# A hybrid decoder layer: where the second half's normalized tokens are transposed

## The chip, the cores and the metric

The kernel runs on one core of one Trainium2 chip. The metric is the device time of one launch in microseconds (us). The median of three runs of the kernel before is 2236.77 us (2235.26 to 2238.23).

## The reference, cut to what matters

Sixteen meta tokens are put ahead of 2048 tokens of 1024 channels (float32). One layer is computed on them:

```python
h = rmsnorm(x, norm_g)                     # per token, over 1024 channels
p = h @ w_in                               # 8208 columns
q, k, v = l2norm/silu of causal_dwconv(p[..., :3072])      # 8 heads x 128
o = chunk_gated_delta_rule(q, k, v, g, beta)               # state 128 x 128 a head
o_dn = rmsnorm(o) * silu(z)
o_sc = b * causal_dwconv(c * hh) * silu(sz)                # 1024 channels
out = rmsnorm(x + concat(o_dn, o_sc) @ w_out, final_g)
```

What this document is about is the first line and its way into the second: the normalized tokens have to stand with the channels on the partitions (h transposed) before the projection can contract over channels.

## The kernel before, in words

The tokens are worked in two halves of 1024 (the first with the 16 meta tokens as well). For each half the transposed, normalized tokens lie in SBUF in two tiles, HH and HL (1024 channels as 8 blocks of 128 partitions, by tokens): HH holds the values rounded to the matmul's float32r format, HL what is left over. Each projection is a "job": 128 columns of `w_in`, split in the same way into `wh` and `wl`, and 24 matmuls for each group of tokens (hh x wh, hl x wh, hh x wl, eight channel blocks each). The first half has three groups of tokens (272, 384 and 384), the second two of 512 (`groups`, lines 365 to 368). Eight slots of eight jobs make a half: q, k, v and the gate z of one head of the delta rule, and four jobs of the short convolution. The second half has the same jobs; its HH and HL are written over those of the first, group by group, once the last two jobs of the first half have read a group (`("free", g)`, line 1517).

Between the matmuls of the jobs runs the delta rule of the heads, as Python generators that are stepped by a planner: `delta_front` (decay, the matrices of key products, a substitution by VectorE), `delta_back` (transposes, the merge of the block inverses), `delta_scan` (the recurrence over eight chunks) and `delta_out`. The planner (`Model`, lines 30 to 100) holds an assumed free time for every engine and a ready time for every tile, and steps a generator when its time has come; so the order of the instructions on TensorE, VectorE, ScalarE and GpSimd is fixed when the program is built. A chip that is later than the plan waits in that order. SP, which issues all DMAs, is not among the engines whose order is fixed by hand (lines 205 to 214).

The second half's tokens are normalized while the first half runs: in each head but the last, `fresh` (line 1065) waits until the scan of the head before is done and then steps `normalize(t)` for one tile of 128 tokens (head 5 has two). `normalize` (line 518) loads the tile into the buffer "kd", takes its mean square on ScalarE (with "gw" for scratch), a power on GpSimd and three small steps on VectorE, multiplies each half of 512 channels by the root and the gain, and stores the tile in DRAM (`xnd`), still with the tokens on the partitions. `delta_back` of the same head starts only when `("fresh", i)` is set, since it uses "kd" as well. "Q" and "gw" are buffers shared with the delta rule and the gates; `hold` (line 571) keeps others off a shared buffer.

At the border `prologue1` (line 544) loads the eight tiles back through three buffers of the short convolution (`sc_c`, `sc_y`, `sc_u`) and calls `turn` (line 383) twice for each tile: four 128 x 128 transposes on TensorE into one of two PSUM buffers "ta", a ScalarE copy into HH and a VectorE subtraction into HL. These sixteen calls stand between the matmuls of the last two jobs of the first half and of the first job of the second. `run_group` (line 736) waits in the plan for `("h", hf, g)`. The weights of the second half's first two jobs are split on GpSimd (`POOLED`), all others on VectorE.

## Time and profile before

| | |
|---|---|
| median of three runs | 2236.77 us |
| profiled execution: its time, its span | 2236.26 us, 2234.5 us |
| mean granted clock of TensorE | 0.992 |
| TensorE busy | 2174.5 us |
| VectorE busy | 1451.7 us |
| ScalarE busy | 854.0 us |
| GpSimd busy | 189.3 us |
| DMA | 197.14 MB in 258366 packets on SP's queue, 46.0% of 16 engines |

The profile is one execution. In it PE is TensorE's matmuls, PEld its weight loads, DVE VectorE, ACT ScalarE, POOL GpSimd and SPq the queue of SP that issues DMAs. An instruction is named by the tiles that it writes and reads (`hl<-ta,hh` writes hl from ta and hh). All instructions have line 118, that of the helper that records them, so they are told apart by their tiles. A number in brackets behind an instruction is the time that its engine stood idle before it, with what ended the wait. The first half's projections run from some 45 us to 951 us, the second half's to some 1930 us, and the output projection fills the rest.

### The profile page before, as it was taken

Reading aid. Unit: us, or ns where it says so; the run is one execution under the profiler, and the core shown is the slowest. Engines: PE = TensorE matmul, PEld = TensorE weight load, DVE = VectorE, ACT = ScalarE, POOL = GpSimd, SP = SyncE. Lnnn points to the kernel's source line nnn. Section 1 sums busy time; section 2 is a strip of 40 time slices with the busy share of each in tenths; the row PEclk is TensorE's granted clock in tenths of the full one; section 3 lists DMA queues with packets and bytes.
Section 4 is the critical chain, followed back from the end, with each engine's and each line's share of the span. In section 5 each row is a group of like instructions: output and inputs, shape, how many; then the busy total and the mean of one; then the engine's idle time right before and its main releaser. Section 6 shows DMA issues by size and latency. Waiting matters only on the chain.

```text
span 2234.5 us, 35464 instructions
## 1 busy us (share of the span) xinstructions
PE 2174.5 (97%) x13472; PEld 1917.1 (86%) x13472; DVE 1451.7 (65%) x3919; ACT 854.0 (38%) x1987; POOL 189.3 (8%) x345
## 2 busy tenths in 40 slices
PE   6999999999998999999999999999999999999998
PEld 6999999999998999977888888888888877888886
DVE  4677777677775668686767677676767674444422
ACT  5533434343443334444344352425252523332211
POOL 4010101010101010111010101010101000000000
PEclk9999999999999999999999999999999999999999
DMA  5434544353446744523444423343677343645521
GB/s 140 76 77 67 86 70 95 64 95 65 92 61 78 83 76 89 131 43 60 82 70 65 83 57 78 53 78 53 79 52 75 60 114 126 203 170 188 188 91 57
DMA packets 258537, 199.41 MB, mean 89 GB/s; under 512 B 62117, under 2 KB 226478, under 8 KB 258366
## 3 DMA queue, kind: packets, MB, share of 16 engines
q1 hardware_dynamic: 258366, 197.14, 46.0%
q8 instruction: 106, 1.74, 0.3%
q14 instruction: 65, 0.53, 0.1%
HBM read 160.51 MB, written 36.59 MB: 88 GB/s over the span
## 4 chain that ended last, share of the span: by engine, by line
PE 88%; DMA 4%; DVE 3%; ACT 2%; SPq 1%; issue 1%; POOL 0%; POOLq 0%; ACTq 0%; DVEq 0%
PE mm L118 75%; PE ta L118 7%; PE rec L118 4%; PE o L118 2%; DMA kd<-in_x_dram 2%; SPq L118 1%; ACT junk L118 1%; DMA wr<-in_w_in_dram 1%; DMA nb<-nbd 1%; DVE prod L118 1%; DMA xtd<-XT 0%; DVE wl L118 0%; DVE XT L118 0%; ACT wh L118 0%; DVE acc L118 0%
## 5 line engine op out<-in xcount | busy, mean ns | idle before, releaser
L118 PE MATMUL mm<-hh,wh 128*128 128x512 f32 (+3 forms) x2816 | 1008.4, 366 | 8.7 <-ACT hh L118 6.7
L118 PE MATMUL mm<-hl,wh 128*128 128x512 f32 (+3 forms) x2816 | 985.4, 357 | 0.4 <-DVE hl L118 0.4
L118 PE MATMUL mm<-hh,wl 128*128 128x512 f32 (+3 forms) x2816 | 640.1, 360 | 1.7 <-DVE wl L118 1.7
L118 PEld LDWEIGHTS mm<-hh,wh 128*128 128x128 f32 x2816 | 533.1, 190 | 60.3 <-ACT hh L118 7.9
L118 PEld LDWEIGHTS mm<-hl,wh 128*128 128x128 f32 x2816 | 532.5, 190 | 48.1 <-DVE hl L118 1.9
L118 PEld LDWEIGHTS mm<-hh,wl 128*128 128x128 f32 x2816 | 479.6, 189 | 48.9 <-DVE wl L118 2.2
L118 DVE TENSOR_TENSOR wl<-wr,wh 128x512 fp32r<-128x512 f32 x356 | 238.3, 689 | 97.6 <-ACT wh L118 77.0
L118 DVE SCALAR_TENSOR_TENSOR acc<-raw,pcol,acc 128x384 f32<-128x384 f32 (+2 forms) x360 | 232.9, 649 | 87.9 <-ACT acc L118 83.8
L118 ACT ACTIVATE wh<-wr 128x1024 fp32r<-128x1024 f32 x182 | 191.9, 1055 | 88.7 <-PE mm L118 49.7
L118 DVE SCALAR_TENSOR_TENSOR prod<-nb,XT 128x8 f32<-128x8 f32 (+30 forms) x496 | 191.0, 385 | 22.7 <-DMA nb<-nbd 19.1
L118 DVE TENSOR_REDUCE XT<-prod 128x8 f32<-128x16 f32 (+30 forms) x496 | 147.2, 297 | 17.0
L118 ACT ACTIVATE vn<-rec,cj 128x128 f32<-128x128 f32 x128 | 46.9, 366 | 248.4 <-PE rec L118 248.1
L118 ACT ACTIVATE raw<-mm 128x384 f32<-128x384 f32 (+2 forms) x120 | 61.5, 513 | 192.7 <-PE mm L118 192.2
L118 PE MATMUL mm<-oh,wh 128*128 128x512 f32 x256 | 101.9, 398 | 0.0
L118 ACT ACTIVATE sc_c<-mm 128x384 f32<-128x384 f32 (+3 forms) x82 | 42.1, 515 | 154.4 <-PE mm L118 154.3
L118 PE MATMUL mm<-ol,wh 128*128 128x512 f32 x256 | 100.4, 392 | 0.0
L118 DVE SCALAR_TENSOR_TENSOR yy<-rec,neg,vr 128x128 f32<-128x128 f32 x128 | 44.5, 348 | 56.1 <-PE rec L118 55.5
L118 DVE TENSOR_TENSOR y<-mm,y 128x512 f32<-128x512 f32 x21 | 14.5, 691 | 101.1 <-PE mm L118 101.1
L118 ACT ACTIVATE ojk<-y 128x512 bf16<-128x512 f32 x21 | 13.2, 631 | 164.6 <-DVE y L118 127.1
L118 DVE SCALAR_TENSOR_TENSOR S<-S,egl,rec 128x128 f32<-128x128 f32 x104 | 35.7, 343 | 59.6 <-PE rec L118 59.1
L118 POOL TENSOR_TENSOR opy<-mo,nhalf 128x4 f32<-128x4 f32 x32 | 34.3, 1073 | 460.3 <-DVE mo L118 451.5
L118 POOL TENSOR_SCALAR_AFFINE_SELECT E<-E 128x1024 f32<-128x1024 f32 x16 | 18.3, 1143 | 641.8 <-PE ta L118 352.3
(240 smaller groups left out, 2574.4 us busy)
## 6 DMA issues: line engine op xcount, KB each, us to landing
wr<-in_w_in_dram SPq DMA_DIRECT2D x128, 512.0 KB, 7.8
wr<-mixd SPq DMA_DIRECT2D x54, 512.0 KB, 4.3
E<-gtd SPq DMA_DIRECT2D x16, 512.0 KB, 3.8
qd<-ged SPq DMA_DIRECT2D x16, 512.0 KB, 6.4
nb<-nbd SPq DMA_DIRECT2D x64, 128.0 KB, 2.8
mixd<-zs SPq DMA_DIRECT2D x32, 256.0 KB, 2.4
out_dram<-y SPq DMA_DIRECT2D x16, 512.0 KB, 2.7
kd<-in_x_dram SPq DMA_DIRECT2D x9, 512.0 KB, 7.6
```

Of the source, the lines that this page charges most:

```text
L118: r = real(*args, **kw)
```

## The change

`xnd` gets another shape: for each tile eight blocks of 128 x 128 with the channels first. `normalize` turns each half of a tile itself: a VectorE block transpose of 128 x 512 (32 x 32 blocks) into the buffer "gw", and four DMAs, each from 32 partitions in runs of 32 elements (128 B), that put the blocks in their transposed place in DRAM. It then lets `DRAIN` (4.0 us of planned time) pass before it lets go of "gw" or goes on, and it holds "gw" against the gates, which now hold it too. At the border `turn` is replaced by `split_h`, which reads the loaded tile in SBUF and has no transposes; the load takes each partition in eight runs of 512 B.

```diff
-    xnd = tc.dram_tile([NC, 128, D], F32, name="xnd")
+    xnd = tc.dram_tile([NC, KT, 128, 128], F32, name="xnd")
...
-    def turn(xt, k0, col, n):
-        pt = ptile(pta, "ta", [128, 4, 128])
-        for k in range(4):
-            kx = 4 * k0 + k
-            tr(pt[:, k, :n], xt[:, kx * 128 : kx * 128 + 128], n)
-        h_ = HH[:, 4 * k0 : 4 * k0 + 4, col : col + n]
-        l_ = HL[:, 4 * k0 : 4 * k0 + 4, col : col + n]
-        nc.scalar.activation(h_, pt[:, :, :n], AF.Copy)
-        nc.vector.tensor_tensor(out=l_, in0=pt[:, :, :n], in1=h_, op=ALU.subtract)
+    def split_h(xt, k0, col):
+        x_ = xt[:, 512 * k0 : 512 * k0 + 512].rearrange("p (k i) -> p k i", i=128)
+        h_ = HH[:, 4 * k0 : 4 * k0 + 4, col : col + 128]
+        l_ = HL[:, 4 * k0 : 4 * k0 + 4, col : col + 128]
+        nc.scalar.activation(h_, x_, AF.Copy)
+        nc.vector.tensor_tensor(out=l_, in0=x_, in1=h_, op=ALU.subtract)
...
     def normalize(i):
...
         yield after(xt)
+        yield from hold("gw")
         st = statistics(xt, 128, vt(dp, [128, 1840], "gw", dt=BF16))
...
             nc.vector.scalar_tensor_tensor(xc, xc, rs, gains[c2], op0=ALU.mult, op1=ALU.mult)
             if c2 == 0:
                 gain(1)
+            else:
+                held.discard("Q")
+            yield after(slot=(dp, "gw"))
+            yield from hold("gw", True)
+            u = vt(dp, [128, 4, 128], "gw")
+            turn_out(xnd[i, 4 * c2 : 4 * c2 + 4], xc.rearrange("p (c i) -> p c i", i=128), u)
+            yield DRAIN
+            held.discard("gw")
+            if c2 == 0:
                 yield after(gains[1])
-        held.discard("Q")
-        nc.sync.dma_start(xnd[i], xt)
         done.add(("xn", i))
...
-            nc.sync.dma_start(xts[i], xnd[i])
+            nc.sync.dma_start(
+                xts[i].rearrange("p (k i) -> p k i", i=128), xnd[i].rearrange("k p i -> p k i")
+            )
...
-                yield after(xts[i], slot=(pta, "ta"), eng="DVE", lag=1.2)
-                yield from hold()
-                turn(xts[i], k0, col, 128)
+                yield after(xts[i], eng="DVE", lag=1.2)
+                split_h(xts[i], k0, col)
...
+    def turn_out(dram, src, tmp):
+        nc.vector.transpose(out=tmp.rearrange("p c i -> p (c i)"), in_=src.rearrange("p c i -> p (c i)"))
+        for a in range(4):
+            nc.sync.dma_start(
+                dram[:, :, 32 * a : 32 * a + 32].rearrange("c (b y) x -> y (c b) x", b=4),
+                tmp[32 * a : 32 * a + 32].rearrange("y c (b x) -> y (c b) x", b=4),
+            )
...
+        yield from hold("gw", True)
         gw = vt(dp, [128, 920], "gw")
...
         nc.sync.dma_start(ged[hf, :Wd], gT[:Wd])
+        held.discard("gw")
...
+    DRAIN = 4.0
```

## Rows read from the trace of the kernel before

**Rows 1.** The page's table: busy time, share, instructions of each engine
```profile
PE 2174.5 (97%) x13472; PEld 1917.1 (86%) x13472; DVE 1451.7 (65%) x3919; ACT 854.0 (38%) x1987; POOL 189.3 (8%) x345
```

**Rows 2.** Busy us (count) by stretch: stretch, length, engines, granted clock, DMA share, GB/s
```profile
60.00:1000.00 940.00, 918.47 (x6565) 881.89 (x6564) 675.01 (x2066) 386.24 (x958) 84.79 (x154) 0.99 0.47 79
...
957.00:965.00 8.00, 7.86 (x35) 6.38 (x36) 6.13 (x25) 2.54 (x5) 1.72 (x5) 0.79 0.54 77
1000.00:1700.00 700.00, 696.65 (x4148) 577.12 (x4147) 492.79 (x1249) 283.58 (x668) 60.14 (x90) 1.00 0.45 69
```

**Rows 3.** Timeline of TensorE around one turn: start, length (us), instruction, count
```profile
935.42 0.60 PE L118 MATMUL ta<-ident,sc_y 128*128 128x128 f32 x4
935.77 0.42 PE L118 MATMUL mm<-hh,wh 128*128 128x384 f32 x1
936.03 0.34 PE L118 MATMUL mm<-hl,wh 128*128 128x384 f32 x1
936.21 0.33 PE L118 MATMUL mm<-hh,wh 128*128 128x384 f32 x1
```

**Rows 4.** Timeline of TensorE, first half's end to group 1; brackets: idle before, releaser
```profile
951.47 0.40 PE L118 MATMUL mm<-hh,wh 128*128 128x512 f32 x1
...
957.00 0.66 PE L118 MATMUL ta<-ident,sc_c 128*128 128x128 f32 x4 [2.87 <-DVE hl L118]
...
970.67 0.39 PE L118 MATMUL mm<-hh,wh 128*128 128x512 f32 x1
```

**Rows 5.** The tile hh: subtractions; ns min/median/max, first and last start
```profile
L118 DVE TENSOR_TENSOR hl<-ta,hh x16: 672/691/693, 927.6 to 963.2; 128x512 fp32r<-128x512 f32 x16
```

**Rows 6.** Timeline of GpSimd and VectorE beside that hole
```profile
949.59 2.70 POOL L118 TENSOR_TENSOR wl<-wr,wh 128x1024 fp32r<-128x1024 f32 x1 [16.39 <-ACT wh L118]
...
950.27 2.04 DVE L118 SCALAR_TENSOR_TENSOR msm<-mnb,mXT 16x5 f32<-16x5 f32 x1
```

**Rows 7.** The page's costliest groups: subtractions that read SBUF alone; mean ns
```profile
L118 DVE TENSOR_TENSOR wl<-wr,wh 128x512 fp32r<-128x512 f32 x356 | 238.3, 689 | 97.6 <-ACT wh L118 77.0
```

**Rows 8.** The tile X: VectorE's block transposes; ns min/median/max
```profile
L118 DVE STREAM_TRANSPOSE X<-W x48: 422/434/440, 209.2 to 1856.3; 32x256 f32<-32x256 f32 x48
```

**Rows 9.** Timeline of SP's queue: four short-run stores
```profile
876.91 1.82 SPq L118 DMA_DIRECT2D xtd<-XT  x4
```

**Rows 10.** DMA issues: count, KB each, median us to landing
```profile
wr<-in_w_in_dram SPq DMA_DIRECT2D x128, 512.0 KB, 7.8
...
xnd<-kd SPq DMA_DIRECT2D x8, 512.0 KB, 2.9
...
xtd<-XT SPq DMA_DIRECT2D x64, 32.0 KB, 4.2
...
sc_c<-xnd SPq DMA_DIRECT2D x3, 512.0 KB, 4.8
```

**Rows 11.** The buffer xtd, first half: its landing times
```profile
DMA to landing us min/median/max: 1.6/1.9/7.6
```

**Rows 12.** VectorE's waits, first half: us in total, times, longest
```profile
DVE pxt L118 <- POOL pxy L118: 17.3, 4, 6.5
...
DVE prod L118 <- DMA nb<-nbd: 10.2, 4, 7.1
```

**Rows 13.** Timeline of TensorE: the two waits that followed from these
```profile
699.22 0.79 PE L118 MATMUL rec<-yy,W 128*128 128x128 f32 x2 [3.63 <-DVE yy L118]
...
724.75 0.66 PE L118 MATMUL rec<-ident,os 128*128 128x128 f32 x4 [3.79 <-DVE os L118]
```

**Rows 14.** Timelines of SP, VectorE and TensorE: head 5's chain, head 7's k job
```profile
756.03 0.33 SPq L118 DMA_DIRECT2D xnd<-kd  x1
...
765.81 3.69 SPq L118 DMA_DIRECT2D xtd<-XT  x4
...
836.90 0.33 DVE L118 SCALAR_TENSOR_TENSOR Sh<-S,egl,rec 128x128 f32<-128x128 f32 x1
...
845.41 0.29 PE L118 MATMUL mm<-hh,wh 128*128 128x272 f32 x1
```

## The prediction

> **What bounds the kernel now.** I read the page's engine table first: TensorE is busy 97% of the span, the next engine, VectorE, 65% [rows 1]. The reader is to see that only time on TensorE's own queue counts, and that an edit elsewhere counts only by the waits that it gives TensorE. The table by stretches comes next: in the first half (60 to 1000 us) TensorE has 21.5 us without work, VectorE is busy 72% of it, and in the second half (1000 to 1700) TensorE lacks 3.4 us in 700 [rows 2]. So the second half follows TensorE closely, and time won at the border between the halves stays won. Then the timeline of TensorE at that border. A turn of half a token tile (four transposes) stands between the projection matmuls sixteen times [rows 3], and one of them is the longest hole there: 2.87 us, which ended with a VectorE subtraction [rows 4]. Behind the hole the granted clock is 0.79 on the mean of 8 us, against 1.00 in the second half [rows 2]; part of that stretch ran at the lower of the two levels (1.2 and not 2.4 GHz), after TensorE had stood idle.
>
> **The change part by part.** All times are those of the profiled execution: 2234.5 us of span, 2236.26 us in all, 0.5 under the median of the three runs.
>
> *Removed from TensorE.* One turn: 0.35 us from its first transpose to the next matmul, and that matmul takes 0.26 where the following step takes 0.18 [rows 3]. That is 0.43, and 16 x 0.43 = 6.9 us. All of it lies on the queue that sets the end; nothing hides it.
>
> *The hole goes.* The turn at 957.00 waited for its PSUM buffer, which VectorE's late subtraction held: 2.87 us. With no transpose there, the matmuls behind it have their inputs and run. The low clock after it goes too: (1 - 0.79) x 8.0 us = 1.7 us [rows 2]. What is late next is group 1 of the second half, whose first matmul is at 970.67 [rows 4] and needs all subtractions of tiles 5 to 7. Before, the last of them started at 963.2 and took 0.69 [rows 5], so it ended 12.4 us after the first half's last column group had let its buffer go (951.47). Ten turns lie ahead of that point, so it comes 4.3 us earlier, at 947.2; 12.4 us later is 959.6. TensorE wants it at 970.67 - 11.5 = 959.2. So even if VectorE takes as long as before, 0.4 us is lost; I count 0. If the hole only moves there, it costs again what it cost, 2.9 + 1.7.
>
> VectorE is slow there because of GpSimd: the 2.70 us weight split on GpSimd stands over a VectorE instruction of 16 x 5 elements that took 2.04 us [rows 6], and a second pair follows 4 us later. The Trainium skill, page SBUF — State Buffer, section Who interferes with whom, says that a VectorE instruction with two SBUF inputs is blocked by a GpSimd instruction that reads SBUF, and that one with a PSUM input isn't. The trace agrees with the first half. It speaks against the change, since the split's subtraction now reads its tile from SBUF and so can itself be blocked; by that rule up to 2 x 2.0 us of delay could fall on the subtractions, which would give back about 4 us at the border.
>
> *The split itself.* ScalarE's copy and VectorE's subtraction stay, 16 of each, from SBUF instead of PSUM: the subtraction from PSUM takes 691 ns, the like one from SBUF 689 [rows 5, 7]. No change; ScalarE likewise.
>
> *Added to VectorE.* Sixteen block transposes of 128 x 512. The trace has 32 x 256 at 434 ns [rows 8]. With twice the elements it lies between 0.43 (all fixed) and 0.87 (all per element); I take 0.87, so 13.9 us over eight tiles. VectorE is idle 28% of the first half, and the projection matmuls hide it: 0 on the path. If that cover fails, it costs at the rate by which VectorE's waits reach TensorE. VectorE waited 17.3 + 10.2 = 27.5 us for late powers and late block loads in the first half, and two TensorE waits, 3.63 + 3.79 = 7.4 us, came of these [rows 12, 13]. The rate is 0.27, so 3.8 us at most.
>
> *Added to SP and the DMA engines.* Per half tile four stores, 64 in all in place of 8. Four stores of the same run length (128 B) take 1.82 us to issue [rows 9], so 16 x 1.82 = 29 us of SP's queue less 8 short ones. SP waits in it for VectorE's transpose, with weight loads behind; they are asked for two jobs ahead, so 0; without that lead, 29 us at the rate above would be 7.7. The store that VectorE waits for is another matter: the second half tile's transpose writes the same buffer, so it waits until the first four stores have landed, and the whole of VectorE's queue stands behind it (scan steps, convolutions), for which TensorE waits at the rate above. The planner lets 4.0 us pass (DRAIN). Landing of the like stores is 4.2 us in the median [rows 10]; that buffer's stores and loads together took 1.6 to 7.6 in the first half [rows 11]. I take 4.2, the row of stores alone; the new ones have twice the bytes. Wait: 1.8 + 4.2 - 4.0 = 2.0 us a tile, 8 x 2.0 x 0.27 = 4.3 us. Ends: 0 (landing 1.6) and 8 x 5.4 x 0.27 = 11.7 (landing 7.6).
>
> 512 KB stored in long runs lands in 2.9 us, 32 KB in 128 B runs in 4.2 [rows 10]. The Trainium skill, DMA: Bandwidth & Descriptors, Specifications, states that below 512 B a transfer is a read-modify-write and misses line rate: the trace agrees in direction. By that rule the end near 11.7 is likelier than 0.
>
> *The loads at the border* now gather 512 B runs, as the weight loads do: 7.8 us to landing, not 4.8 [rows 10]. Only the first tile's has no turn ahead to cover it. ScalarE would wait up to 3.0 us; I take 3.0 x 0.27 = 0.8 (ends 0 and 3.0).
>
> *The normalizing stream gets longer* and delta_back waits for it ("fresh"). Each half tile adds the 4.0 drain and 0.87, so 9.7 a tile. Head 5 has two tiles: its last store, at 756.03, goes to 775.5, past the end of the substitution (765.81 + 3.69 = 769.5) [rows 14]. Head 5's scan then ends 6.0 us later than its 837.2. The slot that needs it, head 7's k job, starts at 845.41 [rows 14]: 8.2 us of slack, so 0. If the slack is gone, each us over it costs TensorE one us, at most 19.5 - 8.2 = 11.3. The other heads have one tile each (head 7 none): 9.7 us, so with no more than head 5's slack 1.5 us each, which I count at 0.
>
> **Sum:** -6.9 - 2.9 - 1.7 + 4.3 + 0.8 = -6.4 us: 2229.9 on the profiled execution, 2230.4 on the median. I forecast 2230.
>
> **Rivals.**
> *Late stores, slower.* Place: VectorE's second transpose of each tile. If landing is 7.6 us at all eight, VectorE waits 5.4, and if TensorE pays as it did for the longest block load (3.63 of 7.1, or 0.51 [rows 12, 13]), 8 x 5.4 x 0.51 = 22 us: 2236.8 - 11.5 + 0.8 + 22 = 2248. It decides from a TensorE loss of 10.7/8 = 1.34 us a tile, which is a VectorE wait of 2.6 and a landing of 4.8 us. For it: twice the bytes of the row, short runs. Against: most like landings before were near 2 us.
> *The first half takes the gain back.* Landing 7.6 at the mild rate 0.27: 2236.8 - 11.5 + 11.7 + 0.8 = 2237.8. The slack of head 7's k job used up gives the same size.
> *The hole stays (the change does not do all it says).* TensorE loses the transposes but waits at 959 for the blocked subtractions or for the late loads of tiles 5 to 7: only 6.9 won, so 2236.8 - 6.9 + 5.1 = 2235. For it: the margin there is nil.
> *Better.* Stores land within the drain, and the new order also dissolves one of the two waits of 3.6 to 3.8: 2236.8 - 11.5 - 3.7 = 2221.6. Against: nothing in the change aims at these waits.
>
> **How the numbers follow.** Forecast 0.44 (own range 2226 to 2232), better 0.14, first half takes it back 0.14, hole stays 0.10, late stores slower 0.18. About 0.2% (4.5 us) is what a measurement can tell from no change. Faster 0.44 + 0.14 = 0.58; same 0.14 + 0.10 = 0.24; slower 0.18. The range 2221 to 2245 leaves out the tip of the better case and the worse half of the slower one.
>
> **What would show it.** Right: no "ta" matmul of sc_c, sc_y or sc_u tiles between the halves, no hole and a granted clock of 1.00 there, the second half's first group at least 9 us earlier against the last one of the first, and VectorE's waits ahead of the new transposes of 2 us or less. Wrong: waits of TensorE on VectorE in the first half that sum to over 7.4 + 11 us, a wait on hh or hl before group 1, or a hole ahead of head 7's k job.

## The result, and the profile after

The changed kernel takes 2265.28 us (median of four runs, 2260.31 to 2269.35) beside 2236.33 of the kernel before on the same chip: ratio 1.0128 [1.0105, 1.015]. It is 29 us slower. I had forecast 2230, and the range ended at 2245.

Everywhere below, single stages come from one profile of each kernel. Two profiles of the same instructions can stand up to 10 us apart at a point (e12 and e13 at 819 us, ahead of all that tells them apart; after and e6, which turn out to be one program, 7.7 us at 1669), so a stage counts only where it recurs in several kernels. The medians carry the verdicts.

**The page of after.** Span 2265.0 us against 2234.5, of which TensorE is busy:

```profile
PE 2189.5 (97%) x13408; PEld 1924.6 (85%) x13408; DVE 1454.7 (64%) x3931; ACT 850.9 (38%) x1985; POOL 190.7 (8%) x345
```

The 64 transposes are gone (13408 matmuls for 13472 in [rows 1]), and yet TensorE is busy 15.0 us longer and idle 15.5 us longer (75.5 for 60.0). Busy time grows with fewer instructions when the clock is lower. The mean granted clock fell from 0.992 to 0.982. Clock loss, (1 - clock) x span with the clocks unrounded, is 40.2 us after and 17.0 before: 23 us more. The table by stretches shows where:

```profile
60.00:1000.00 940.00, 909.67 (x6420) 874.27 (x6419) 662.46 (x2040) 377.07 (x948) 84.94 (x154) 0.97 0.51 79
782.00:866.00 84.00, 78.69 (x562) 73.26 (x561) 53.52 (x176) 37.27 (x104) 8.42 (x16) 0.90 0.49 80
780.00:800.00 20.00, 19.54 (x95) 17.54 (x95) 11.50 (x24) 9.21 (x33) 1.38 (x3) 0.70 0.74 69
...
968.00:1030.00 62.00, 56.85 (x246) 41.93 (x246) 50.38 (x171) 23.41 (x44) 3.88 (x7) 0.92 0.29 47
1000.00:1700.00 700.00, 694.39 (x4077) 570.04 (x4076) 489.60 (x1234) 280.35 (x649) 54.52 (x79) 0.99 0.46 66
1660.00:1680.00 20.00, 17.85 (x145) 13.47 (x144) 9.15 (x16) 6.52 (x12) 0.19 (x1) 0.64 0.29 49
```

The granted clock is the last number but two. In the first half it is 0.97, where before had 0.99 [rows 2]. The stretches from 782, 968 and 1660 are the ones where this profile of after loses its time: (1 - 0.90) x 84 = 8.4 us of clock, 5.0 and 7.2. The kernel before ran 780 to 800 and 1660 to 1680 at 1.00 with TensorE 20.00 of 20 us busy.

**The waits ahead of those stretches.** TensorE's timeline of after (start, length, instruction; in brackets the idle time before it and who ended it), which answers to [rows 4, 13]:

```profile
715.16 0.79 PE L118 MATMUL rec<-S,k 128*128 128x128 f32 x2 [5.79 <-DVE S L118]
...
779.36 0.55 PE L118 MATMUL mm<-hh,wh 128*128 128x256 f32 x1 [4.12 <-DVE sc_y L118]
...
856.58 0.65 PE L118 MATMUL rec<-S,k 128*128 128x128 f32 x2 [1.09 <-DVE S L118]
...
945.56 0.80 PE L118 MATMUL rec<-yy,W 128*128 128x128 f32 x2 [3.11 <-DVE yy L118]
...
974.32 0.49 PE L118 MATMUL rec<-S,k 128*128 128x128 f32 x2 [1.63 <-DVE S L118]
976.15 0.75 PE L118 MATMUL rec<-yy,W 128*128 128x128 f32 x2 [1.12 <-DVE yy L118]
...
1664.97 0.22 PE L118 MATMUL ta<-X,E 32*32 32x32 f32 x2 [1.33 <-issue]
```

The hole on hl at 957.00 is gone, as forecast; these stand in its place. They are short, and where a stretch at a low clock follows, it can cost more than the wait (1660 to 1680: 2.15 us of waits, 7.2 us of clock). On S, yy, sc_y, X and wl of VectorE, TensorE waited 23.1 us between 60 and 1000 us (10.2 + 5.3 + 4.1 + 1.8 + 1.7): over the 18.4 that the prediction had named as the sign that it is wrong. By the same count before has 15.4, on os, yy, hl and wl.

**The parts that I had priced.** The tiles hl and gw and the DMA issues of after [rows 5, 8, 10], then VectorE's waits on DMAs and GpSimd over the whole span [rows 12]:

```profile
L118 DVE STREAM_TRANSPOSE gw<-kd 128x512 f32<-128x512 f32 x16 | 11.3, 708 | 1.2 <-DMA xnd<-gw 1.0
```
```profile
L118 DVE TENSOR_TENSOR hl<-sc_c,hh x6: 672/682/692, 938.0 to 976.0; 128x512 fp32r<-128x512 f32 x6
```
```profile
Q<-in_norm_g_dram SPq DMA_DIRECT2D x16, 256.0 KB, 3.9
...
xnd<-gw SPq DMA_DIRECT2D x64, 64.0 KB, 3.0
```
```profile
DVE prod L118 <- DMA nb<-nbd: 26.3, 7, 9.6
DVE kd L118 <- DMA Q<-in_norm_g_dram: 19.3, 4, 10.5
...
DVE gw L118 <- DMA xnd<-gw: 1.0, 2, 0.6
DVE pxt L118 <- POOL pxy L118: 0.3, 1, 0.3
```

The wait that I priced highest, VectorE on the landing of the first four stores, is 1.0 us in all, not 8 x 2.0. In its place VectorE waits 19.3 us, in four waits, for the second gain load, which it had hardly waited for before. The block transpose takes 0.71 us.

**Head 5's chain** [rows 14], SP's queue and VectorE's timeline of after:

```profile
754.79 4.01 SPq L118 DMA_DIRECT2D wr<-in_w_in_dram  x2
760.87 0.35 SPq L118 DMA_DIRECT2D Q<-in_norm_g_dram  x1
761.62 19.36 SPq L118 DMA_DIRECT2D xnd<-gw  x8
```
```profile
747.71 0.75 DVE L118 SCALAR_TENSOR_TENSOR kd<-kd,pxr,Q 128x512 f32<-128x512 f32 x1 [5.74 <-DMA Q<-in_norm_g_dram]
...
776.35 0.75 DVE L118 SCALAR_TENSOR_TENSOR kd<-kd,pxr,Q 128x512 f32<-128x512 f32 x1 [10.48 <-DMA Q<-in_norm_g_dram]
```

The last store of head 5's second tile is issued by 781, against 756.03. I had worked out 775.5 with 2.2 us to spare; the two waits on gain loads, 16.2 us, were not in it. The second of these gain loads is issued at 760.87, right behind two weight loads, and lands at 776.33, 15.5 us later, where 3.9 is the median of such loads. In before, SP's queue has it ahead of the weight load:

```profile
750.54 0.33 SPq L118 DMA_DIRECT2D Q<-in_norm_g_dram  x1
754.60 0.38 SPq L118 DMA_DIRECT2D wr<-in_w_in_dram  x1
```

The scans, counted by ScalarE's vn, are 11.8 to 16.8 us late at the starts of heads 1 to 4, 23.2 at head 5's and 28.5 at head 6's, and TensorE waits for them from 853 to 859 and from 974 to 982 us.

**How stages are lined up.** ScalarE's 120 records of acc (one per column group of q, k or v that leaves TensorE) are complete in every profile, so the shift of the n-th against before tells how late a kernel is there. Where an order moves other work across such a point, a part of the shift is that work and no loss. The stages in the expectations were lined up by a count of TensorE's mm records that was not complete (every trace holds 9296 of them) and drifted: they put 16 us on after's stage from 782 to 850 us, where the table has 8.2 from 819 to 948. The table is the corrected one. Shifts in us; the columns are the time in before.

| kernel | 726 | 819 | 948 | 971 | 1070 | 1611 | 1669 | span |
|---|---|---|---|---|---|---|---|---|
| after | +1.6 | +3.8 | +12.0 | +19.6 | +18.1 | +21.5 | +30.5 | +30.5 |
| e1_border_only | +3.0 | +3.3 | -2.6 | -2.8 | -9.3 | +1.0 | +11.1 | +3.9 |
| e8_quarter_turns | +3.1 | +3.5 | -1.4 | -2.2 | +1.2 | +6.3 | +5.7 | +9.0 |
| e2_first_half_only | -2.0 | +2.0 | +9.7 | +11.5 | +13.7 | +16.0 | +21.2 | +14.9 |
| e3_spread | +7.8 | +1.5 | +2.5 | +10.5 | +9.0 | +13.3 | +26.7 | +20.2 |
| e4_gains_first | +6.0 | +7.9 | +13.6 | +21.4 | +20.7 | +30.6 | +33.2 | +35.8 |
| e6_no_drain | -0.8 | +3.2 | +12.2 | +19.7 | +18.3 | +21.7 | +22.8 | +27.1 |
| e7_long_runs | +1.0 | +4.3 | +13.4 | +21.6 | +20.3 | +23.7 | +23.9 | +21.9 |
| e5_before_spread | -3.6 | -4.9 | -6.2 | -6.3 | -5.1 | -1.0 | +10.3 | +3.7 |
| e15_spread_order_kept | -0.1 | +0.1 | -2.7 | -2.7 | +0.1 | +4.4 | +15.6 | +10.6 |
| e9_border_order_kept | +5.2 | +6.3 | +3.1 | +4.5 | +7.2 | +7.2 | +7.7 | +5.7 |
| e16_border_small_turns | +3.9 | +2.2 | +1.6 | +1.3 | +1.3 | +2.0 | +1.6 | +1.6 |
| e12_no_lows | +5.6 | +9.6 | +5.4 | -0.5 | +1.1 | +1.1 | +1.4 | +1.8 |
| e13_before_no_lows | -0.1 | +0.1 | -0.2 | -5.2 | -3.6 | -3.5 | -3.9 | -3.7 |
| e11_first_order_kept | +3.2 | +5.3 | +5.3 | +6.3 | +9.1 | +9.9 | +9.3 | +7.3 |
| e10_all_order_kept | +6.7 | +10.0 | +6.7 | +7.1 | +7.1 | +7.1 | +8.6 | +7.6 |
| e18_all_small_turns | +2.7 | +2.4 | +1.8 | +1.5 | +4.2 | +4.6 | +6.8 | +10.9 |
| e14_lows_on_pool | +8.1 | +11.3 | +10.6 | +14.2 | +14.2 | +14.2 | +15.5 | +17.6 |
| e17_before_extra_turns | +1.7 | +1.1 | +12.0 | +15.9 | +17.6 | +17.5 | +16.9 | +16.2 |

After loses 8.2 us from 819 to 948, 7.6 at the border and 9.0 from 1611 to 1669. The first two are there in e6 and e7 as well, which have after's order, and the third is not. The first thing that the table shows is that the second half runs in step once the order of before is kept: in the nine kernels of its last rows, from e9 on, the shift at 1070 is still there at 1611, within 0.8.

### The profile page after: what moved, and what is told of

It is laid out like the page before. It is cut to its first block, busy times and chain, and to the rows that moved or that the text cites. A ratio compares the mean times of both kernels' runs of the same rounds, so it can differ in the third digit from the quotient of the medians.

```text
span 2265.0 us, 35410 instructions
## 1 busy us (share of the span) xinstructions
PE 2189.5 (97%) x13408; PEld 1924.6 (85%) x13408; DVE 1454.7 (64%) x3931; ACT 850.9 (38%) x1985; POOL 190.7 (8%) x345
## 3 DMA queue, kind: packets, MB, share of 16 engines
q8 instruction: 105, 1.72, 0.3%
## 4 chain that ended last, share of the span: by engine, by line
PE 87%; DMA 5%; DVE 3%; ACT 2%; SPq 2%; issue 1%; POOL 0%; POOLq 0%; DVEq 0%; ACTq 0%
PE mm L118 74%; PE ta L118 7%; PE rec L118 4%; PE o L118 2%; SPq L118 2%; DMA nb<-nbd 1%; ACT junk L118 1%; DMA wr<-in_w_in_dram 1%; DMA xnd<-gw 1%; DMA sc_y<-xnd 0%; DVE prod L118 0%; DVE acc L118 0%; DVE wl L118 0%; DVE hl L118 0%; DMA W<-xtd 0%
## 5 line engine op out<-in xcount | busy, mean ns | idle before, releaser
L118 PE MATMUL mm<-hh,wh 128*128 128x512 f32 (+3 forms) x2816 | 1009.5, 366 | 16.8 <-ACT hh L118 11.3
L118 ACT ACTIVATE ojk<-y 128x512 bf16<-128x512 f32 x22 | 13.9, 631 | 174.0 <-DVE y L118 127.2
L118 ACT ACTIVATE acc<-mm,pcol 128x384 f32<-128x384 f32 (+2 forms) x120 | 71.9, 599 | 0.0
L118 POOL TENSOR_TENSOR kpy<-ssk,nhalf 128x8 f32<-128x8 f32 x16 | 28.2, 1764 | 516.3 <-DVE ssk L118 454.0
```

Source lines behind the costliest of these rows:

```text
L118: r = real(*args, **kw)
```

## The experiments

Medians; "before" is the kernel before on the same chip (2236.1 to 2237.8).

**First: which half of the change costs it?** Theory A: the longer normalizing makes head 5 late. Theory B: the short-run stores hold up the loads beside them.

*e1_border_only*: the kernel before with the split from SBUF in place of the turn, and its plain store and load.

```diff
-                turn(xts[i], k0, col, 128)
+                split_h(xts[i], k0, col)
```


> The kernel before, with only the border changed: tiles are normalized, stored and loaded as before (not transposed; so the second half is computed from tokens whose blocks are not turned), and split_h takes the place of turn. No short-run stores, no longer normalizing stream. Theory A (the longer normalizing stream makes head 5's chain late) and theory B (the short-run stores hold up the gain and block loads) both put the whole loss into the first half, so both expect the border's gain alone: 2236.3 - 6.9 (transposes) - 4.6 (hole and low clock) = about 2225, and no hole of over 1 us at the border. If the border itself is at fault, this stays at 2236 or above.

Measured 2242.41, ratio 1.0025 [1.0015, 1.0035]: 17 us above what I expected. The half that had to win, alone, loses. At 1070 us it is 9.3 us ahead; from 1070 to 1669 it loses 20. Some 7 us of both are work that its order puts off: between the two records next to 1070 and 1611 us TensorE is busy 548.1 us in e1 and 540.7 in before, both at a clock of 1.00. From 1669 to the end 7.2 us come back.

*e2_first_half_only*: the normalizing of after with its stores to a place that nothing reads, beside the plain store; the border of before.

```diff
+            turn_out(xnd[i, 4 * c2 : 4 * c2 + 4], ..., u)
+            yield DRAIN
...
+        nc.sync.dma_start(xnp[i], xt)
...
-            nc.sync.dma_start(xts[i], xnd[i])
+            nc.sync.dma_start(xts[i], xnp[i])
```


> The changed kernel with the border of before: the transposes and the 64 short-run stores are made (into DRAM that nobody reads), and the tile is also stored as before, loaded as before and turned by TensorE. Theories A and B: the whole loss stays and the border's gain is missing, so 2265 + 7 to 11 = 2272 to 2276, with TensorE's hole ahead of head 7's k job. If the loss comes from the border, about 2236 to 2242.

Measured 2250.76, 1.0073 [1.0056, 1.009]: the first half costs 14 us alone, less than expected. 14.3 + 6.0 is not 29, so the halves don't simply add.

*e3_spread*: after, with no head that normalizes two tiles but head 0.

```diff
-            news = ((0,), (1,), (2,), (3,), (4,), (5, 6), (7,), ())[i] if hf == 0 else ()
+            news = ((0, 1), (2,), (3,), (4,), (5,), (6,), (7,), ())[i] if hf == 0 else ()
```


> The changed kernel with the second tile moved from head 5 to head 0 (tiles 0 and 1 in head 0, then one in each head up to 6), so that no head but the first, which has about 40 us of cover, normalizes two. Same instructions, same stores. Theory A: head 5's scan ends at about 845 or earlier instead of 860, TensorE's waits there and the low clock go, -13 to -16 us: about 2250. Theory B: same stores, same late loads, so within 5 us of 2265.

Measured 2256.34, 1.0096 [1.0081, 1.0111]: 9 us under after. The loss from 819 to 948 falls from 8.2 to 1.0, as theory A says; the 8.0 at 948 to 971 and 13.4 from 1611 stay.

*e4_gains_first*: after, with both halves of a tile scaled before either is transposed.

```diff
+                yield after(gains[1])
+        held.discard("Q")
+        for c2 in range(2):
+            xc = xt[:, 512 * c2 : 512 * c2 + 512]
```


> The changed kernel with both halves of a tile scaled first and both transposes and their stores after them, so that the second half's gain is loaded ahead of the stores. Theory B: VectorE's waits for the gain load fall from 19.3 us to under 2, and the time to about 2255. Theory A: the stream is as long as before (only the waits inside move), head 5 is as late, 2262 to 2268.

Measured 2272.75, 1.0179 [1.0156, 1.0201]: 7 us slower than after. VectorE's waits on gain loads fell to 8.3 us and it gained nothing by it. But the order is another one too, so this does not clear the gain loads.

**Second: the order.** What stands out is that kernels which differ little lose at places where nothing of theirs was changed. Every instruction is placed by the planner's own clock, so one edit moves all behind it. Theory C: the new order is what costs.

*e5_before_spread*: the kernel before with e3's table (the same one-line edit).

> The kernel before, with nothing but the places of its normalized tiles moved as in e3_spread: head 0 takes two tiles, heads 1 to 6 one each, instead of two at head 5. Theory A (in the kernel after, the longer normalizing at head 5 uses up the slack of head 7's k job; in the kernel before, that slack is there): no change, 2232 to 2238 us, since the stage from 782 to 850 us has only 0.8 us of idle to give. Theory C (any new order of the instructions breaks up the order of before and makes new short waits of TensorE, each followed by a stretch at the lower clock): slower by 0.3% or more, 2243 to 2256 us, like the parts of e3_spread that lie outside that stage.

Measured 2238.31, 1.0 [0.999, 1.0011]. A new order need not cost. But a loss from 1611 to 1669 is there (+11.3), in a kernel without any part of the change, and up to 1070 it is ahead. From 1669 to the end 6.6 us of it come back.

*e6_no_drain*: after without the pauses.

```diff
-    DRAIN = 4.0
+    DRAIN = 0.0
```


> The kernel after, with the pause of 4 us that each half of a tile keeps behind its stores set to 0, so that a tile's normalizing is up to 8 us shorter and gives the buffer gw back before its stores have landed. Theory A (length of the normalizing stream at head 5): head 5's two tiles end 16 us earlier, the stage from 782 to 850 us falls from +16 us to under +5, the time to about 2250 to 2255 us; who takes gw next waits up to 3 us for the stores. Theory B (the stores' traffic delays the loads of gains and blocks): the same traffic, only earlier, 2260 to 2270 us. Theory C (the order alone): anywhere from 2255 to 2275 us, with the loss moved to other stages.

Measured 2262.96, 1.0116 [1.0098, 1.0134]. The edit moved nothing: in the traces of e6 and of after, the instructions of all four engines and SP's DMAs stand in the same order (13408 on TensorE, 3931 on VectorE). So the pauses cost nothing, theory A was not tested by this, and e6 is after once more. Two profiles of one program tell what belongs to its order. The losses from 819 to 948 (8.2 in after, 9.0 in e6) and from 948 to 971 (7.6, 7.5) and the waits on gain loads (19.3, 20.6 us) recur. The loss from 1611 to 1669 doesn't (9.0, 1.1): where after waits 1.33 and 0.82 us and then runs at 0.64, e6 waits 0.95 and 0.60 and runs at 1.00.

```profile
1660.00:1680.00 20.00, 18.45 (x179) 14.54 (x178) 12.76 (x24) 10.81 (x20) 0.19 (x1) 1.00 0.51 60
```

*e7_long_runs*: after, with the stores in runs of 2 KB.

```diff
-                dram[:, :, 32 * a : 32 * a + 32].rearrange("c (b y) x -> y (c b) x", b=4),
-                tmp[32 * a : 32 * a + 32].rearrange("y c (b x) -> y (c b) x", b=4),
+                dram[a].rearrange("(y z) x -> y (z x)", z=4), tmp[32 * a : 32 * a + 32].rearrange("y c i -> y (c i)")
```


> The kernel after, but each of the four stores of a half tile writes its 32 partitions as whole rows of 2 KB to another place, so that the border loads tokens that are not turned rightly (their values are misplaced; the same bytes, instructions and pauses, only the runs of 128 bytes gone). Theory B (the short runs of the stores delay the loads beside them): the four waits of VectorE on the second gain load fall from 19.3 us to under 5, its waits on block loads from 26.3 to about 19, and the time to 2245 to 2252 us. Theory A (the longer stream with its transposes and pauses): those waits may fall, but the stage from 782 to 850 us keeps most of its +16 us, 2258 to 2268 us.

Measured 2258.95, 1.0094 [1.0079, 1.0109]: 6.3 us under after and 4.0 under e6, with the same order of the compute engines' instructions. So by the medians the short runs cost 4 to 6 us at most, and the intervals of the ratios meet. VectorE's waits are as in after:

```profile
DVE prod L118 <- DMA nb<-nbd: 24.8, 7, 9.4
DVE kd L118 <- DMA Q<-in_norm_g_dram: 22.4, 4, 12.2
```

Theory B falls: it is not the short runs that the gain loads wait for. The Trainium skill, DMA: Bandwidth & Descriptors, Specifications, states that a transfer under 512 B misses line rate. Here 64 KB landed in 3.0 us in the median in 128 B runs and in 2.5 in 2 KB runs (e7): the direction agrees. But 3.0 is under the 4.2 of the 32 KB in 128 B runs that the kernel before already has [rows 10], so the rule did not decide the landing that I had let it speak on.

*e8_quarter_turns*: before with one transpose for each turn instead of four.

```diff
-        for k in range(4):
-            kx = 4 * k0 + k
-            tr(pt[:, k, :n], xt[:, kx * 128 : kx * 128 + 128], n)
+        tr(pt[:, 0, :n], xt[:, 512 * k0 : 512 * k0 + 128], n)
+        pt = pt[:, 0:1].to_broadcast([128, 4, 128])
```


> The kernel before, with one transpose on TensorE for each half tile at the border instead of four; the other three blocks are copies of the first (tokens left out). It takes 48 transposes of about 0.108 us off TensorE, 5.2 us, and adds no instruction to any other place. If TensorE's time at the border counts as it stands: 2231 us (2230 to 2233). If it is given back later, because the second half's first heads wait for a chain that did not come earlier (what e1_border_only showed after 1015 us), or because the order changes: 2234 to 2244 us.

Measured 2244.64, 1.003 [1.0018, 1.0043]. Five us of TensorE less, and it is 7 us slower. Its order differs from before's too, on VectorE from 928 us on. From here the question was whether time on TensorE at the border is worth anything at all.

**Third: the change with the order of before.** The planner is charged for what it no longer issues, and not told of what is new, so every instruction stands where it stood.

*e9_border_order_kept*: e1 in the order of before.

```diff
+        pt = Ghost()
+        model.tile(pta, "ta", nbufs[id(pta)], pt)
+        for k in range(4):
+            model.issue("PE", 0.109, [pt], [xt, ident])
...
+        tc.nc.scalar.activation(h_, x_, AF.Copy)
+        model.issue("ACT", ..., [h_], [pt])
+        tc.nc.vector.tensor_tensor(out=l_, in0=x_, in1=h_, op=ALU.subtract)
+        model.issue("DVE", 0.066 + 512 / 960.0, [l_], [pt, h_])
```


> e1_border_only (the border without TensorE's turns, the tokens loaded unturned, so with misplaced values), but the planner is charged for the 64 transposes that are no longer issued, and for the split as before, so that every engine's instructions stand in the order of the kernel before, less the turns. Theory C (what e1 lost after 1015 us was its new order): the gain stays, 2225 to 2229 us, and the stages after 1015 us are within 3 us of before's. Theory D (time that TensorE wins at the border is lost again in the second half, whatever the order, because VectorE's and the DMAs' chains do not come earlier): 2235 to 2243 us, with new waits of TensorE between 1015 and 1680 us.

Measured 2241.3, 1.0018 [1.0008, 1.0028]: no gain in before's own order either. From 819 to 1070 it loses 0.9 where 11.5 were to be won. After 1070 nothing more is lost, so theory D's "lost again in the second half" is wrong too: the time is not won in the first place. The table by stretches (950 to 970 us) and two timelines of e9, TensorE and VectorE, show why:

```profile
950.00:960.00 10.00, 10.00 (x51) 9.02 (x50) 9.79 (x31) 6.83 (x19) 6.13 (x3) 1.00 0.67 185
960.00:970.00 10.00, 3.89 (x14) 2.99 (x14) 9.18 (x35) 3.61 (x7) 4.51 (x5) 0.83 0.42 64
```
```profile
967.47 1.11 PE L118 MATMUL rec<-ident,os 128*128 128x128 f32 x4 [6.11 <-DVE os L118]
```
```profile
956.59 2.26 DVE L118 SCALAR_TENSOR_TENSOR msm<-mnb,mXT 16x6 f32<-16x6 f32 x1
...
961.21 0.67 DVE L405 TENSOR_TENSOR hl<-sc_u,hh 128x512 fp32r<-128x512 f32 x1
...
962.43 1.28 DVE L405 TENSOR_TENSOR hl<-sc_c,hh 128x512 fp32r<-128x512 f32 x2
...
964.28 1.28 DVE L405 TENSOR_TENSOR hl<-sc_y,hh 128x512 fp32r<-128x512 f32 x2
...
966.72 0.69 DVE L118 TENSOR_TENSOR os<-os,so 128x512 f32<-128x512 f32 x1
```

VectorE (the third busy time) has hardly any idle time left there, and TensorE runs into it: the hole of 2.87 us on hl [rows 4] is now one of 6.11 on os, which stands in VectorE's queue behind the subtractions, and at 0.83 of the clock. At the border it is VectorE that is late. Of its time ahead of this os, 4.3 us are two instructions of 16 x 5 and 16 x 6 elements beside GpSimd's two weight splits, where the median of the 128 like them is 0.146 us:

```profile
953.60 2.03 DVE L118 SCALAR_TENSOR_TENSOR msm<-mnb,mXT 16x5 f32<-16x5 f32 x1
```
```profile
956.42 2.41 POOL L118 TENSOR_TENSOR wl<-wr,wh 128x1024 fp32r<-128x1024 f32 x1 [0.82 <-ACT wh L118]
```

Before has two of this kind as well, 2.04 [rows 6] and 1.98 us. Not all that reads two SBUF inputs is held up: prod<-nb,XT took 0.27 at 953.13, beside a split that the profile has from 952.66. Whether the border's time would be won with these splits off GpSimd was not tried.

*e11_first_order_kept*: e2 in the order of before.

```diff
+            u = dp.tile([128, 4, 128], F32, tag="gw", name="gw")
+            turn_out(xnd[i, 4 * c2 : 4 * c2 + 4], xc.rearrange(...), u)
```


> e2_first_half_only (the border as before; the 16 VectorE transposes and their 64 short-run stores go to a place that nothing reads, beside the plain store), but the planner is not told of the transposes and stores and has no pauses behind them, so that every other instruction stands in the order of the kernel before. VectorE does 11.4 us more (16 x 0.71) and may wait for the first four stores of a tile. Theory A (the work and the stores themselves make head 5 late): the stage from 782 to 850 us keeps 10 us or more, 2246 to 2255 us. Theory C (the pauses and the new order made it): 2236 to 2241 us, the stage within 4 us of before's.

Measured 2242.91, 1.0024 [1.0014, 1.0034]: 6.1 us instead of 14.3, between the two forecasts. The waits on gain loads are gone, with the same stores and transposes in place. VectorE's waits (the first is on the blocks of head 5's and others' chain, the second on the stores that I had priced at 16 us), and TensorE:

```profile
DVE X L118 <- DMA W<-xtd: 6.6, 3, 5.5
...
DVE gw L585 <- DMA xnd<-gw: 2.0, 3, 0.8
```
```profile
785.06 1.48 PE L118 MATMUL ta<-X,E 32*32 32x32 f32 x32 [4.43 <-issue]
```

*e10_all_order_kept*: both, that is the whole change in the order of before.

```diff
+            turn_out(xnd[i, 4 * c2 : 4 * c2 + 4], xc.rearrange(...), u)
...
-        nc.sync.dma_start(xnd[i], xt)
+        model.issue("DMA", 128 * D * 4 / 36e4, [xnp[i]], [xt])
```


> The whole change, with the order of the kernel before kept by both means of e9_border_order_kept and e11_first_order_kept (nothing left out). Theory C (the order): 2225 to 2234 us, faster than before. Theories A and D together (the work itself): 2250 to 2266 us, as the kernel after. If the two halves add, it is 2236 plus what e9_border_order_kept and e11_first_order_kept each differ from it.

Measured 2246.27, 1.0045 [1.003, 1.006]: 9.4 us above before, and 4.5 + 6.1 = 10.6 would be the sum of e9 and e11. So the halves add once the order is held, and of after's 29 us the new order makes about 19 (2265.3 - 2246.3, taken against two medians of before 0.5 apart). Theory C holds for two thirds of the loss, though not with its number (2225 to 2234): with the order kept, the change still costs 9. The scan steps of the second half in after and e10 (the first start is what is to be read):

```profile
L118 DVE SCALAR_TENSOR_TENSOR S<-Sh,egl,rec x8: 336/347/349, 1162.9 to 1908.0; 128x128 f32<-128x128 f32 x8
```
```profile
L118 DVE SCALAR_TENSOR_TENSOR S<-Sh,egl,rec x8: 342/346/348, 1151.9 to 1886.4; 128x128 f32<-128x128 f32 x8
```

From the second half's first scan step to the end of the span is 1102.1 us in after, 1098.6 in e6 and 1090.2 in e10 (before: 1089.8). Some 11 of the 23 us between the profiles of after and e10 are lost ahead of it, 12 behind; e6 has 8 of these 12.

**Fourth: is VectorE what takes the border's gain?** Theory E.

*e12_no_lows*: e9 without the 16 subtractions; *e13_before_no_lows*: before without them.

```diff
-        tc.nc.vector.tensor_tensor(out=l_, in0=x_, in1=h_, op=ALU.subtract)
```
```diff
-        nc.vector.tensor_tensor(out=l_, in0=pt[:, :, :n], in1=h_, op=ALU.subtract)
+        model.issue("DVE", 0.066 + 512 / 960.0, [l_], [pt, h_])
```


> e9_border_order_kept without the 16 subtractions of VectorE that make the low parts at the border (0.68 us each, 10.9 us; the low parts of the first half's tokens stay in their place). Theory E (at the border VectorE is the late engine: it was 9.2 to 9.8 of 10 us busy from 950 to 970 us, and TensorE waited 6.1 us for its os): the wait goes, head 7's chain comes earlier, the turns' 6.9 us are won, 2224 to 2231 us. Theory D (the second half's chain comes when it comes): 2236 to 2242 us.

> The kernel before, with TensorE's turns and with its order, but without the same 16 subtractions (0.69 us each, 11.1 us; low parts left out). Theory E: the hole of 2.87 us at 957.00 goes and VectorE's chain of head 7 comes earlier, 2227 to 2233 us; what e12_no_lows is below this is what TensorE's turns cost once VectorE is not in the way, 5 to 8 us. Theory D: 2235 to 2240 us, and no gain from the turns on top.

Measured e12 2235.05, 0.9989 [0.9975, 1.0004]; e13 2232.69, 0.9981 [0.9968, 0.9994]. Taking 11 us off VectorE wins 6.3 us on e9 and 3.4 on before, where taking 6.9 off TensorE won nothing: in these profiles VectorE is the later of the two. The hole on os shrinks with it (e12):

```profile
965.23 0.66 PE L118 MATMUL rec<-ident,os 128*128 128x128 f32 x4 [1.56 <-DVE os L118]
```

But the forecast that the turns are then worth 5 to 8 us is missed: e12 is not under e13. From 819 to 1070 e12 gains 8.5 us and e13 3.7, which would make the turns worth 4.8; e12's profile had come to 819 us 9.6 us late, ahead of the border. The intervals meet, so this stays open.

*e14_lows_on_pool*: e10 with the subtractions on GpSimd.

```diff
-        tc.nc.vector.tensor_tensor(out=l_, in0=x_, in1=h_, op=ALU.subtract)
+        tc.nc.gpsimd.tensor_tensor(out=l_, in0=x_, in1=h_, op=ALU.subtract)
```


> e10_all_order_kept with the border's 16 subtractions on GpSimd instead of VectorE (nothing left out). Theory E: VectorE gets 10.9 us back, and GpSimd, which is 85% idle there, takes 16 x about 1.5 to 2.7 us: 2234 to 2241 us, below e10_all_order_kept's 2246. Rival: GpSimd's low parts come later than the groups that read them and slow VectorE beside them: new waits of TensorE on hl, 2248 to 2262 us.

Measured 2252.67, 1.0065 [1.0045, 1.0086]: the rival. GpSimd takes 1.33 us for one, and TensorE's hole grows:

```profile
L406 POOL TENSOR_TENSOR hl<-sc_y,hh 128x512 fp32r<-128x512 f32 x6 | 7.9, 1329 | 2.0 <-ACT hh L403 1.9
```
```profile
977.97 1.12 PE L118 MATMUL rec<-ident,os 128*128 128x128 f32 x4 [9.07 <-DVE os L118]
```
```profile
958.59 1.31 DVE L118 SCALAR_TENSOR_TENSOR prod<-nb,XT 128x56 f32<-128x56 f32 x1
...
976.20 1.72 DVE L118 TENSOR_TENSOR os<-os,so 128x512 f32<-128x512 f32 x1
```

VectorE's own instructions took 1.31 and 1.72 us beside it, 0.69 for the same os in e9. The Trainium skill, SBUF — State Buffer, Who interferes with whom, states that a VectorE instruction with two SBUF inputs contends with a GpSimd instruction that reads SBUF; these rows agree. The work was moved off VectorE, and a part of it came back as longer instructions.

*e15_spread_order_kept*: e10 with e3's table.

> e10_all_order_kept with the tiles spread as in e5_before_spread (head 0 takes two, heads 1 to 6 one each), the order being that of e5_before_spread less the turns; nothing left out. Theory A (what e11_first_order_kept costs, 6 us, is the two tiles at head 5): the first half costs nothing, and it comes out at e5's 2238 plus the border's 4.5: 2238 to 2244 us. If the stores and the block transposes cost the same wherever they stand: 2245 to 2252 us.

Measured 2246.65, 1.0041 [1.0029, 1.0053], no better than e10: the rival. It has e5's order, so e5 is what it is to be held against, and there the change costs 10 us (10.5 above before, e5 0.6), as in before's order (9.4). Theory A falls: it isn't the two tiles at head 5. Against e5 it is 3.5 us late at 726, 5.2 at 1070 and 5.3 at 1669; the 11.2 from 1611 to 1669 are e5's own. In this table, too, the planner's order costs more: e3, the same change and table in the order that the planner makes for it, is 9.7 us slower than e15.

**Fifth: a loss ahead of the border.** e1, e8, e9 and e12 are 3 to 5.6 us late at 726 us, where they are the kernel before, instruction by instruction. All have fewer instructions of TensorE later on. Theory F: the number of these instructions moves it.

*e16_border_small_turns* and *e18_all_small_turns*: e9 and e10 with the transposes put back at 32x32; *e17_before_extra_turns*: before with a transpose of 32x32 ahead of each of its own.

```diff
+            tr(pt[:32, k, :32], xt[:32, kx * 128 : kx * 128 + 32], 32)
```
```diff
+            tc.nc.tensor.transpose(out=pt[:32, k, :32], in_=xt[:32, kx * 128 : kx * 128 + 32], identity=ident[:32, :32])
             tr(pt[:, k, :n], xt[:, kx * 128 : kx * 128 + 128], n)
```


> e9_border_order_kept with the 64 transposes put back in their places at a sixteenth of their size (32x32, about 0.02 us each by the row of ta<-X, 1.5 us in all; nothing reads them), so that TensorE has as many instructions as before. Theory F (5 of e9's 4.5 us are lost ahead of the border, at 700 to 730 us, where its instructions are the same as before's, and come with the number of TensorE's instructions; the border itself gives 0.7): the shift at 726 us is under 1 us, 2233 to 2238 us. Rival (the border costs it): 2240 to 2243 us.

> The kernel before, with 64 more transposes of 32x32 on TensorE beside the border's own (nothing reads them; 1.5 us of TensorE, in a place where the kernel before has a hole). Theory F: another number of TensorE's instructions moves the waits of 700 to 730 us, 2240 to 2243 us, with a shift of 3 us or more at 726 us. Rival (the number is of no account; what e1, e8, e9 and e12 lost there is chance or comes from the border): 2236 to 2239 us, with a shift under 1 us at 726 us.

> e10_all_order_kept (the whole change in the order of before) with the same small transposes at the border; nothing left out. Theory F: about 5 us below e10's 2246, 2239 to 2243 us; rival: 2245 to 2249 us.

Measured e16 2237.76, 1.0004 [0.9995, 1.0012]; e17 2251.32, 1.0065 [1.0053, 1.0077]; e18 2245.49, 1.0034 [1.002, 1.0047]. Theory F falls: e16 with the full number is 3.9 us late at 726, e17 with more only 1.7, and e18 is no better than e10. What moves that stage is not known. e16 is weaker at the border than I meant it to be. Its turn still holds TensorE's queue for 0.32 us of the 0.43 (0.22 to the next matmul, and 0.28 for that one where 0.18 is usual). With that 1.8 us taken off, the time is that of before and the hole on os is there already:

```profile
965.49 0.66 PE L118 MATMUL rec<-ident,os 128*128 128x128 f32 x4 [3.01 <-DVE os L118]
```

e17 shows the other side. Its small transposes cost far more than I had put down, since each breaks the row of large ones:

```profile
927.48 0.20 PE L388 MATMUL ta<-ident,sc_c 32*32 32x32 f32 x1
927.61 0.33 PE L118 MATMUL ta<-ident,sc_c 128*128 128x128 f32 x1
927.86 0.20 PE L388 MATMUL ta<-ident,sc_c 32*32 32x32 f32 x1
927.99 0.33 PE L118 MATMUL ta<-ident,sc_c 128*128 128x128 f32 x1
```

A pair takes 0.38 us where one large transpose took about 0.1, so 64 x 0.28 = 18 us were added to TensorE, and 14 us came out at the end. Time added to TensorE at the border is paid nearly in full (e17); time taken off it is not won (e9, e16). That VectorE right behind it is the reason is what the profiles show; by the medians it stays open, since e12, with VectorE relieved as well, is not under e13.

No kernel that leaves nothing out is faster than the one before. The whole change at its best is 8 to 9 us slower (e18, e10).

## Why the prediction was wrong

*TensorE's time at the border is won (-6.9), the hole goes (-2.9) and its low clock (-1.7).* This is the step that gave the sign, and it failed. The instructions went as worked out; their time did not. I had even priced the other way ("if the hole only moves there, it costs again what it cost") and then left it at 0 on a count of when TensorE wants the subtractions of group 1. That count looked at one consumer of VectorE's queue. The one that was late is another, os, which the planner puts behind the subtractions. Measured with the order kept: +4.5 us (e9), of which the stretch from 819 to 1070 us has 0.9, where 11.5 were to be won; the rest its profile lost ahead of the border, and the cause of that is open. What I had feared from GpSimd, the subtractions blocked, did not come (0.67 to 0.69 us each in e9). The two small instructions that its splits had held up before are held up again, ahead of this os. The reading behind it was too coarse: 72% busy for VectorE over the first half [rows 2] hides 9.3 to 9.8 of 10 us from 950 to 970.

*What is won at the border stays won.* This held: with the order kept, the shift at 1070 us is the shift at 1611.

*VectorE's wait for the landing of the stores (+4.3).* Mis-sized: 1.0 us of wait in all (2.0 in e11) instead of 16. The new stores land in 3.0 us in the median, within the 4.0 that I had set against it, and the slower rival built on them (2248) fell although its side was right.

*The block transposes, 13.9 us beside the matmuls, SP's queue, the chain of head 5: all at 0.* With the order kept, these cost 6.1 us together (e11). SP's short-run stores stand ahead of head 5's own stores there, its blocks come back late (5.5 us of VectorE's wait), TensorE waits 4.43. With e5's order the whole change costs 10 us, with before's 9.4, so this does not hang on head 5 alone. That the stores do it is read from the queue's order and was not tried by itself. The transposes' duration was within the bounds (0.71 between 0.43 and 0.87). For the loads at the border (+0.8) ScalarE waited once, 4.0 us in after, for the second tile; what that cost TensorE no run separates.

*Head 5's slack.* I had 6.0 us late against 8.2 of slack. After is some 25 late at the last store, because the normalizing stream also waits for its gain loads, 5.74 and 10.48 us, and heads 1 to 4, which I had counted at 9.7 us each, start up to 16.8 us late already. e3, which takes the second tile from head 5, wins 9 us and the loss of that stage, in an order that differs elsewhere too; in before's order the two tiles stand at head 5 as well, and the shift stays as it is from 819 to 948 (e11: 5.3, 5.3). So two tiles at head 5 cost this stage in after's order and not in before's. Why the gain loads are late is read and not tried: the second one stands behind two weight loads in SP's queue, in e6 and e7 as in after. It isn't the short runs (e7), and in another order they are on time with the same stores in place (e11).

*The term that was missing.* The planner places every instruction by its own clock, and the holds and costs of the change move that clock (the pauses moved nothing: e6); which of them does it was not taken apart. About 19 of the 29 us come from the order so made (after against e10), and with e3's table about 10 of 20 (e3 against e15). I had taken the order as fixed and summed edits upon it. The 9 us from 1611 to 1669 do not belong to the order: e6 and e7 have the same one and lose 1.1 and 0.2 there.

*The price of a wait.* I took low clock as 1.7 us on one hole. In after there are 15.5 us more of idle time and 23 more of clock loss, less the 6.9 of transposes: waits of 1 to 6 us each, and around them stretches at 0.64 to 0.92.

## What to carry to other kernels

Before time is taken off the engine that bounds a kernel, look at that place, in windows of 10 us, for the engine that is next, and go through all that stands in its queue there, not through the one result that the edit touches. Where a planner orders the instructions, separate the edit from the order: charge the planner for the old costs and issue the new instructions, and the edit's own price stands by itself. Line up two traces by records that both have in full, check the count first, and check that no work has moved across the mark. Before a stage of a profile is explained, take a second profile of the same program: the 9 us from 1611 to 1669 in after were not there in e6.

## What the runs showed of the hardware

- A 32x32 transpose between two of 128x128 adds 0.28 us to TensorE's queue each time (e17), while four of them in a row hold it for 0.22 us (e16).
- Idle TensorE can be paid twice. After's 15.5 us of added idle time come with 23 us of added clock loss: 780 to 800 us ran at a granted clock of 0.70 behind a wait of 4.12, 1660 to 1680 at 0.64 behind waits of 1.33 and 0.82. The same instructions in e6 waited 0.95 and 0.60 and ran on at 1.00.
- A VectorE block transpose of 128x512 takes 0.71 us, less than twice the 0.43 of 32x256 [rows 8].
- A VectorE instruction of 16 x 6 elements took 2.26 us beside GpSimd's weight split of 2.41 (e9); the median of the 128 like it is 0.146.
- A gain load of 256 KB issued right behind two weight loads landed in 15.5 us (after; 16.2 in e6, 18.1 in e7); the median of such loads is 3.9.
- Kernels with the same instructions up to 819 us reach it up to 9.5 us apart in their profiles (e12 against e13; 5.7 at 726). Whether that is chance or belongs to the kernel was not settled; the number of TensorE's instructions does not decide it (e16, e17).
